# Second layer's attention: later-block sums on VectorE, one triangle product per bank, a bf16 mask, and paired scores

## The chip, the cores and the metric

The kernel runs on one core of one Trainium2 chip. The metric is the device time of one execution in microseconds (us); the median of several runs counts. The core has a matrix engine (TensorE; PE in the profile, PEld for its weight loads), a vector engine (VectorE, DVE), a scalar engine (ScalarE, ACT), GpSimd (POOL) and a queue engine (SyncE, SP) that issues most of the transfers. Matmuls write to PSUM banks of 512 float32 per partition.

## What is computed

Two transformer blocks over 512 tokens of width 1024. The first one (gated linear attention, sliding-window attention and a PEER layer that retrieves single-neuron experts for each token) stays as it is. The change touches the two attentions of the second block, which work on eight stick-breaking heads of width 64 and four differential heads of two scores each:

```python
def one_block(args):                       # stick-breaking, per block of 128 queries
    z = jnp.einsum('bqhd,bkhd->bhqk', qb, k).astype(jnp.float32) * scale
    mask = (k_pos[None, :] < q_pos[:, None])[None, None]
    log_1mb = jnp.where(mask, jax.nn.log_sigmoid(-z), 0.0)
    rem = lax.cumsum(log_1mb, axis=3, reverse=True) - log_1mb
    a = jnp.where(mask, jnp.exp(jax.nn.log_sigmoid(z) + rem), 0.0)
    return jnp.einsum('bhqk,bkhd->bqhd', a.astype(v.dtype), v)

def one_block(args):                       # differential
    logits = jnp.einsum('bqhcd,bkhcd->bhcqk', qb, k).astype(jnp.float32) * scale
    ...
    p = jax.nn.softmax(logits, axis=-1)
    attn = p[:, :, 0] - lam * p[:, :, 1]
    return jnp.einsum('bhqk,bkhd->bqhd', attn.astype(v.dtype), v)
```

Behind the attentions come an output projection, a gated feed-forward of width 2816 and two residual sums.

## The kernel before, in words

Activations lie transposed, features on partitions and tokens along the free axis. The second block is computed in two parts: tokens 0 to 383 as soon as their first block is done (`attend(0, 3, ..., "a", True)`, line 2219), and tokens 384 to 511 later (`attend(3, 4, ub, "b", False)` in `last_block`, line 2197), since the PEER layer gathers the experts of those last 128 tokens row by row (`sparse`, line 1213: indirect transfers issued by POOL, dot products and sums on VectorE, tiles `row` and `vacc`). The weights of part "a" are split into an upper and a lower half (`whi`, `wlo`) and multiplied three times in a reduced format (one record each in the trace); part "b" multiplies in full float32 (two records each).

The order of all instructions is made when the kernel is built. Work is written as generators; a `Weaver` (line 229) always continues the one that its `Model` of the engines (line 70) holds to be ready first, with a handicap given in us where one is set (`(biases(), 8.0)`). A generator gives up its turn at each `yield`; `need(k)` waits for a key that another one sets with `W.set(k)`, `data(t)` for a tile to be loaded. On the chip each engine then works through its instructions in that order, and semaphores make it wait for data and buffers. `stream` (line 1612) feeds the weight tiles: the projections into query, key and value, the output projection and the feed-forward. It takes the pieces of part "b" first when their inputs are there, and else those of "a".

PSUM is laid out in line 1568: two banks `mm` for `stream`, two `w` (scores and transposes of the differential heads, and the sums of squares of all norms, `rstd_bcast`, line 458), two `z` for the stick-breaking scores, one each for the two outputs.

Stick-breaking (`stick`, line 1806): key blocks of 128 are grouped from the last backwards, as many as fit in one bank of 512 columns (`groups`, `offs`, line 1793). In part "a" the blocks 2 and 1 (128 and 256 query columns) make the first group and block 0 (384) the second; in part "b" all four blocks (128 each) make one group. `front` (line 1809) multiplies keys by queries into a bank, and makes the negative log of 1 - beta out of it (ScalarE and VectorE, tile `L`), with a strict mask `sgt` on the diagonal blocks. `back` (line 1830) adds into the same bank, for each key block, a triangle product with its own `L`, a product of all ones with the `L` of every later block, and on diagonal blocks a product of the unit matrix with a mask of -1e30; ScalarE then takes the exponential and the result is multiplied by the values. The core of it:

```python
for jb in jbs:
    o, m = offs[jb]
    PE.matmul(z[:, o:o + m], tri[:, 0], L[h, g][:, o:o + m], stop=False, **kw)
    for j2 in range(jb + 1, b1):
        o2, m2 = offs[j2]
        PE.matmul(z[:, o + m - m2:o + m], tri[:, 1], L[h, where[j2]][:, o2:o2 + m2], stop=False, **kw)
    if 128 * jb >= c0:
        PE.matmul(z[:, o:o + 128], ident, tri[:, 2], stop=True, **kw)
```

Each unit's `front` is emitted ahead of the `back` of the unit before.

Differential (`diff`, line 1874): for a head and a block of 128 queries, `front` (line 1878) multiplies the two 64-feature halves, which lie on partitions 0 to 63 and 64 to 127, each into a `w` bank, with a `yield` between the matmul and VectorE's pass that adds the bias and takes the maximum; `back` (line 1897) normalises, transposes and multiplies by the values. There are 12 units in part "a" (128, 256 and 384 keys for each of four heads) and 4 in part "b" (512 keys).

`biases` (line 1581) loads the position bias of the four heads and masks a corner of each with a memset. `last_feed` (line 2115) is the feed-forward of part "b" and ends the kernel.

## Time and profile before

| | |
|---|---|
| median of 3 runs | 2201.95 us (2199.81 to 2206.16) |
| the profiled execution | 2213.97 us, span from first to last instruction 2212.2 us |
| busy share of the span | PE 91%, PEld 80%, DVE 81%, ACT 44%, POOL 30% |
| instructions | PE 11845, DVE 3705, ACT 1800, POOL 523 |
| mean granted TensorE clock | 0.958 of full speed |
| HBM | 611.54 MB read, 24.38 MB written, 287 GB/s over the span |

All rows come from that one profiled execution. Times are us from the start of the span unless a unit stands beside them. Every instruction carries line 224, that of a helper through which all are recorded, so the rows are told apart by engine, operation and tile: `b_z<-L,tri` is a matmul with `tri` as the stationary and `L` as the moving operand into a bank `b_z`. Matmuls are pipelined: the time that one takes from the engine is the distance of its start to the start of the next, and not its duration.

### The profile page before, as it was taken

The page shows a single profiled execution, that of the slowest core. Times are in us where ns is not written, and L with a number is a line of the kernel's source. Part 1 is how long each engine was busy: PE and PEld are TensorE (multiplying, and loading weights), DVE is VectorE, ACT ScalarE, POOL GpSimd, SP SyncE. Part 2 cuts the span into 40 slices and gives each one's busy share as a digit, 9 for nine tenths or more (in the row PEclk, how much of TensorE's full clock was granted, in tenths as well). Part 3 has the DMA queues.
Part 4 walks back from the last instruction along what each step waited for, and adds up shares of the span by engine and source line. Part 5 has one row for each costly group of instructions (what it writes and reads, how often), then busy time and mean ns, then how long its engine had stood idle before and what let it go on. Part 6 is the DMA issues. An engine that isn't in the chain of part 4 may idle for free.

```text
span 2212.2 us, 33369 instructions
## 1 busy us (share of the span) xinstructions
PE 2014.6 (91%) x11845; PEld 1774.7 (80%) x11845; DVE 1791.9 (81%) x3705; ACT 964.3 (44%) x1800; POOL 656.0 (30%) x523
## 2 busy tenths in 40 slices
PE   2889799798999977899999999799988999999998
PEld 2778676587889866799998998587767999998987
DVE  7846887789999877899898898888889999724577
ACT  1331442212587433444445544444554333344466
POOL 0000222432212234444343344345543555200000
PEclk9899899699999988999999999999999999999999
DMA  9963447898899999999999899688866999742587
GB/s 367 350 210 122 156 137 225 273 334 314 293 312 315 327 326 333 360 391 375 354 370 358 326 394 337 231 299 304 272 218 201 350 375 377 268 156 92 179 285 273
DMA packets 226311, 638.13 MB, mean 288 GB/s; under 512 B 21041, under 2 KB 70465, under 8 KB 226145
## 3 DMA queue, kind: packets, MB, share of 16 engines
q1 hardware_dynamic: 152416, 367.54, 47.0%
q0 software_dynamic: 73728, 268.47, 34.2%
q8 instruction: 93, 1.52, 0.3%
q14 instruction: 74, 0.60, 0.1%
HBM read 611.54 MB, written 24.38 MB: 287 GB/s over the span
## 4 chain that ended last, share of the span: by engine, by line
PE 47%; DVE 22%; DMA 12%; issue 11%; POOL 5%; ACT 2%; SPq 0%; POOLq 0%; DVEq 0%; ACTq 0%
PE b_mm L224 29%; PE b_dacc L224 7%; POOL row L224 5%; DVE row L224 4%; PE b_z L224 4%; PE b_w L224 4%; DMA row<-peer_v,eU 3%; DVE o L224 3%; DMA wraw<-peer_v 3%; DVE vacc L224 2%; DVE wlo L224 2%; PE b_osb L224 1%; DMA row<-w_down 1%; DMA row<-peer_u,eU 1%; PE b_odf L224 1%
## 5 line engine op out<-in xcount | busy, mean ns | idle before, releaser
L224 POOL DMA_INDIRECT row<-peer_u,eU x256 | 328.0, 1281 | 802.0 <-DVE row L224 260.7
L224 POOL DMA_INDIRECT row<-peer_v,eU x256 | 325.2, 1270 | 440.9 <-DVE row L224 198.9
L224 PE MATMUL b_mm<-u,whi 128*128 128x384 f32 x1216 | 326.9, 349 | 11.0 <-ACT u L224 2.4
L224 PE MATMUL b_mm<-h,whi 128*128 128x256 f32 (+2 forms) x1648 | 332.0, 296 | 3.1 <-ACT whi L224 2.4
L224 DVE SCALAR_TENSOR_TENSOR vacc<-row,dots,vacc 128x1024 f32<-128x1024 f32 x254 | 325.2, 1280 | 5.5 <-DMA row<-peer_v,eU 5.0
L224 DVE SCALAR_TENSOR_TENSOR row<-row,h2n 128x1024 f32<-128x1024 f32 x256 | 310.5, 1218 | 10.5 <-DMA row<-peer_u,eU 10.1
L224 PEld LDWEIGHTS b_mm<-h,whi 128*128 128x128 f32 (+1 forms) x1648 | 271.3, 189 | 24.4 <-issue 6.9
L224 PE MATMUL b_mm<-h,wlo 128*128 128x256 f32 (+2 forms) x824 | 242.6, 294 | 13.5 <-DVE wlo L224 13.5
L224 PEld LDWEIGHTS b_mm<-u,whi 128*128 128x128 f32 x1216 | 221.6, 192 | 30.0 <-issue 5.8
L224 PE MATMUL b_mm<-u,wlo 128*128 128x384 f32 x608 | 206.9, 340 | 2.5 <-DVE wlo L224 2.5
L224 ACT ACTIVATE whi<-wraw 128x1024 fp32r<-128x1024 f32 (+3 forms) x129 | 125.5, 973 | 186.9 <-PE b_mm L224 147.1
L224 ACT ACTIVATE vhi<-wraw 128x1024 fp32r<-128x1024 f32 x128 | 135.8, 1062 | 148.6 <-PE b_dacc L224 82.8
L224 PE MATMUL b_dacc<-vhi,ghi 128*128 128x512 f32 x512 | 166.5, 407 | 31.2 <-ACT ghi L224 31.1
L224 PE MATMUL b_mm<-h,uraw 128*128 128x256 f32 x704 | 166.3, 385 | 4.7 <-DMA uraw<-peer_uT 3.3
L224 PEld LDWEIGHTS b_mm<-h,wlo 128*128 128x128 f32 (+1 forms) x824 | 156.1, 189 | 15.9 <-DVE wlo L224 14.8
L224 PE MATMUL b_dacc<-vlo,ghi 128*128 128x512 f32 x512 | 164.4, 403 | 1.4 <-DVE vlo L224 1.4
L224 PE MATMUL b_dacc<-vhi,glo 128*128 128x512 f32 x512 | 162.4, 399 | 0.0
L224 DVE TENSOR_TENSOR vlo<-wraw,vhi 128x1024 fp32r<-128x1024 f32 x128 | 156.2, 1220 | 3.6 <-PE b_dacc L224 2.2
L224 PEld LDWEIGHTS b_mm<-h,uraw 128*128 128x128 f32 x704 | 131.6, 194 | 21.4 <-issue 3.7
L224 DVE TENSOR_TENSOR wlo<-wraw,whi 128x1024 fp32r<-128x1024 f32 (+3 forms) x129 | 143.4, 1113 | 4.2 <-ACT whi L224 2.3
L224 DVE TENSOR_TENSOR wlo<-uraw,whi 128x1024 fp32r<-128x1024 f32 x84 | 103.2, 1229 | 44.3 <-ACT whi L224 42.0
L224 PEld LDWEIGHTS b_dacc<-vhi,ghi 128*128 128x128 f32 x512 | 93.3, 195 | 50.7 <-ACT ghi L224 36.2
(371 smaller groups left out, 3734.4 us busy)
## 6 DMA issues: line engine op xcount, KB each, us to landing
uraw<-peer_uT SPq DMA_DIRECT2D x128, 512.0 KB
wraw<-peer_v SPq DMA_DIRECT2D x128, 512.0 KB
wraw<-w_in SPq DMA_DIRECT2D x60, 512.0 KB
row<-w_ada SPq DMA_DIRECT2D x48, 512.0 KB
wraw<-w_peer_q SPq DMA_DIRECT2D x32, 512.0 KB
gt<-gate_d SPq DMA_DIRECT2D x16, 1024.0 KB
gate_d<-stg SPq DMA_DIRECT2D x16, 896.0 KB
row<-w_in SPq DMA_DIRECT2D x24, 512.0 KB
```

Of the source, the lines that this page charges most:

```text
L224: return f(*args, **kw)
```

## The change

Four edits in the second block's attention, and two that make room.

- Sums of later blocks: in `front`, running sums of `L` over the later key blocks are made on VectorE (tile `Ss`), so that in `back` each key block takes one product of all ones for each piece of the sum in place of one for each later block.
- The triangle product is issued once for the whole bank.
- The mask of -1e30 and the unit matrix it is multiplied by are kept in bf16 (`hide`, `identb`); `biases` converts them, ahead of the bias loads, and `stick` waits for it.
- Both score matmuls of a differential unit are issued one behind the other, into two banks, with one `yield` behind both.
- The tile `fN` of `operands` now lies in the ring `sba`; `tri` has two parts in place of three.

```diff
--- before.py
+++ after.py
@@ -1572,13 +1572,21 @@
     pK = stK.enter_context(tc.tile_pool(name="pK", bufs=1))
     sk, dk = [pK.tile([128, 4, T], F32, name=n) for n in ("sk", "dk")]
     sv, dv = [pK.tile([128, 4, 512], F32, name=n) for n in ("sv", "dv")]
-    tri = pK.tile([128, 3, 128], F32, name="tri")
-    SP.dma_start(tri, A["tri"])
+    tri = pK.tile([128, 2, 128], F32, name="tri")
+    SP.dma_start(tri, A["tri"][:, 0:2])
+
+    hide, identb = [pK.tile([128, 128], BF, name=k) for k in ("hide", "identb")]
+    hide32 = pU.tile([128, 384], F32, name="sqs", bufs=2)[:, :128]
+    SP.dma_start(hide32, A["tri"][:, 2])
     sgt = pK.tile([128, 128], F32, name="sgt")
     SP.dma_start(sgt, A["sgt"])
     bias = pK.tile([128, 4, 512], F32, name="bias")
 
     def biases():
+        yield data(hide32)
+        DVE.tensor_copy(hide, hide32)
+        DVE.tensor_copy(identb, ident)
+        W.set("hide")
         for h in range(4):
             src = bass.AP(tensor=line.tensor, offset=line[h].offset + 127, ap=[[639, 128], [1, 512]])
             SP.dma_start(bias[:, h], src)
@@ -1731,7 +1739,7 @@
                     act(q, x[:, kc], AF.Square)
                     PE.matmul(ps, ones, q, start=(kc == 0), stop=(kc == KC - 1))
                     yield
-                f = pD.tile([128, n], F32, name="fN", bufs=1)
+                f = pD.tile([128, AW], F32, name="sba", bufs=3)[:, :n]
                 act(f, ps, AF.Ln, scale=1.0 / D, bias=eps)
                 act(f, f, AF.Exp, scale=-0.5)
                 yield
@@ -1804,7 +1812,7 @@
         AW = max(w for _, w in groups)
 
         def stick():
-            Z, L, po = {}, {}, {}
+            Z, L, po, later, now = {}, {}, {}, {}, {}
 
             def front(h, g):
                 j, r = h // 2, slice(64 * (h % 2), 64 * (h % 2) + 64)
@@ -1827,20 +1835,31 @@
                         d = l[:, offs[jb][0]:offs[jb][0] + 128]
                         tt(d, d, sgt, OP.mult)
 
+                run = now.setdefault(h, [])
+                for jb in jbs:
+                    o, m = offs[jb]
+                    later[h, jb] = run
+                    new, a0 = [], n - m
+                    for v, a, b in run if jb else ():
+                        t = pD.tile([128, b - a], F32, name="Ss", bufs=2 * max(1, b1 - 2))
+                        tt(t, v, l[:, o + a - a0:o + b - a0], OP.add)
+                        new.append((t, a, b))
+                    e = run[0][1] if run else n
+                    run = ([(l[:, o:o + e - a0], a0, e)] if e > a0 else []) + new
+                now[h] = run
+
             def back(h, g):
                 j, r = h // 2, slice(64 * (h % 2), 64 * (h % 2) + 64)
                 jbs, w = groups[g]
                 z = Z.pop((h, g))
-                where = {jb: gi for gi, (js, _) in enumerate(groups) for jb in js}
                 kw = dict(start=False, skip_group_check=True)
+                PE.matmul(z[:, :w], tri[:, 0], L[h, g], stop=False, **kw)
                 for jb in jbs:
                     o, m = offs[jb]
-                    PE.matmul(z[:, o:o + m], tri[:, 0], L[h, g][:, o:o + m], stop=False, **kw)
-                    for j2 in range(jb + 1, b1):
-                        o2, m2 = offs[j2]
-                        PE.matmul(z[:, o + m - m2:o + m], tri[:, 1], L[h, where[j2]][:, o2:o2 + m2], stop=False, **kw)
+                    for v, a, b in later.pop((h, jb)):
+                        PE.matmul(z[:, o + m - n + a:o + m - n + b], tri[:, 1], v, stop=False, **kw)
                     if 128 * jb >= c0:
-                        PE.matmul(z[:, o:o + 128], ident, tri[:, 2], stop=True, **kw)
+                        PE.matmul(z[:, o:o + 128], identb, hide, stop=True, **kw)
                 yield
                 a = pD.tile([128, AW], F32, name="sba", bufs=3)[:, :w]
                 act(a, z[:, :w], AF.Exp)
@@ -1860,6 +1879,7 @@
             for q in ("sq0", "sk0", "sv0"):
                 yield need(q + tag)
             yield need("xn")
+            yield need("hide")
             yield from front(*units[0])
             for i, (h, g) in enumerate(units):
                 if i + 1 < len(units):
@@ -1880,12 +1900,14 @@
                 p = pD.tile([128, 2, KW], F32, name="dp", bufs=2)
                 m = pD.tile([128, 4], F32, name="dm", bufs=2)
                 P[i, h] = (p, m)
-                for cc in range(2):
+
+                pss = [bank(), bank()]
+                for cc, ps in enumerate(pss):
                     r = slice(64 * cc, 64 * cc + 64)
-                    ps = bank()
                     PE.matmul(ps[:, :nk], dq[r, h, 128 * (i - b0):128 * (i - b0) + 128], dk[r, h, :nk],
                               start=True, stop=True)
-                    yield
+                yield
+                for cc, ps in enumerate(pss):
                     DVE.tensor_tensor_reduce(p[:, cc, :nk], ps[:, :nk], bias[:, h, 512 - nk:], 1.0, -3.0e38,
                                              OP.add, OP.max, m[:, cc:cc + 1])
                 DVE.tensor_scalar(m[:, 0:2], m[:, 0:2], -1.0, None, op0=OP.mult)
```

## Rows read from the trace of the kernel before

**Rows 1.** Busy us by stretch: PE, PEld, DVE, ACT, POOL; clock, DMA share, GB/s

```profile
1469.00:1645.00 176.00, 165.92 (x828) 128.64 (x827) 150.56 (x279) 92.61 (x198) 89.95 (x73) 0.96 0.79 267
...
1700.00:1905.00 205.00, 200.46 (x1150) 198.78 (x1149) 196.56 (x220) 70.01 (x92) 115.70 (x93) 1.00 0.97 357
...
1930.00:2055.00 125.00, 124.40 (x919) 112.70 (x918) 42.31 (x84) 54.60 (x135) 0.00 (x0) 1.00 0.39 123
...
2111.00:2207.00 96.00, 91.91 (x613) 81.71 (x612) 77.66 (x81) 66.74 (x78) 0.00 (x0) 1.00 0.87 303
```

**Rows 2.** TensorE's weight-load queue, what it waited for, 1469 to 1660: us, times, longest

```profile
PEld b_w L224 <- ACT ns L224: 3.3, 3, 2.7
```

**Rows 3.** The same of TensorE's matmuls, 1905 to 2084

```profile
PE b_mm L224 <- DVE wlo L224: 1.5, 3, 0.7
```

**Rows 4.** Matmuls by group, 2055 to 2212: count, busy us, mean ns

```profile
L224 PE MATMUL b_mm<-fh,whi 128*128 128x384 f32 x80 | 20.9, 340 | 0.1
...
L224 PE MATMUL b_mm<-u,whi 128*128 128x384 f32 x35 | 9.1, 339 | 0.0
```

**Rows 5.** Chain of work that ended last: start, us, what

```profile
1470.48 4.39 PE b_mm L224 x24
```

**Rows 6.** TensorE in order of time: start, us to last end

```profile
2084.89 1.05 PE L224 MATMUL b_osb<-ident,xT 128*128 128x128 f32 x8
...
2109.95 0.51 PE L224 MATMUL b_mm<-fh,whi 128*128 128x384 f32 x2
```

**Rows 7.** TensorE in order of time, one head of stretch B

```profile
2000.06 2.17 PE L224 MATMUL b_z<-L,tri 128*128 128x128 f32 x18
2002.07 0.61 PE L224 MATMUL b_mm<-u,row 128*128 128x128 f32 x4
```

**Rows 8.** TensorE in order of time, one score of stretch B

```profile
2019.25 1.12 PE L224 MATMUL b_w<-dk,mix 64*128 64x512 f32 x2
2020.31 0.61 PE L224 MATMUL b_mm<-u,whi 128*128 128x384 f32 x2
```

**Rows 9.** On the tile tri: count, shortest, median, longest ns, first start

```profile
L224 PE MATMUL b_z<-tri,ident x64: 275/275/421, 1476.2 to 2038.8; 128*128 128x128 f32 x64
```

**Rows 10.** TensorE in order of time, stretch A, scores of the differential heads

```profile
1565.70 1.43 PE L224 MATMUL b_w<-dk,mix 64*128 64x384 f32 x4
...
1581.87 0.48 PE L224 MATMUL b_w<-dk,mix 64*128 64x128 f32 x2
1582.29 0.86 PE L224 MATMUL b_osb<-sba,sv 128*64 128x128 f32 x4
...
1627.69 0.49 PE L224 MATMUL b_w<-dk,mix 64*128 64x128 f32 x4
1628.11 0.86 PE L224 MATMUL b_osb<-sba,sv 128*64 128x384 f32 x2
...
1641.44 1.62 PE b_w L224 x2
```

**Rows 11.** Instructions on the tile sgt

```profile
L224 DVE TENSOR_TENSOR L<-L,sgt x32: 285/292/295, 1472.7 to 2032.5; 128x128 f32<-128x128 f32 x32
```

**Rows 12.** SyncE's queue in order of time

```profile
1417.52 1.85 SPq L224 DMA_DIRECT2D bias<-line  x4
1428.18 43.12 SPq L224 DMA_DIRECT2D wraw<-w_in  x8
```

**Rows 13.** Instructions on the tile bias

```profile
L224 DVE CUSTOM_DVE_ANT_0 dp<-b_w,bias x32: 282/488/693, 1479.4 to 2022.9; 128x128 f32<-128x128 f32 x8, 128x256 f32<-128x256 f32 x8, 128x384 f32<-128x384 f32 x8, 128x512 f32<-128x512 f32 x8
...
L224 DVE MEMSET bias<- x4: 112/112/112, 1426.9 to 1448.2; 64x64 f32 x4
```

**Rows 14.** TensorE in order of time, the last expert sum

```profile
1907.22 1.09 PE L224 MATMUL b_w<-ident,vacc 128*128 128x128 f32 x8 [1.02 <-DVE vacc L224]
```

**Rows 15.** VectorE, what it waited for, 1469 to 1660

```profile
DVE L L224 <- ACT sba L224: 9.6, 7, 2.4
DVE dp L224 <- PE b_w L224: 8.3, 8, 2.3
```

## The prediction

> **What bounds the kernel now.** I read the busy time by stretch first [rows 1]. Call 1469 to 1700 us stretch A (attention of the first 384 tokens, beside which the first layer still gathers experts for the last 128) and 1930 to 2055 stretch B (attention of those last 128 tokens). In B TensorE is busy 124.40 of 125.00 us at a granted clock of 1.00, VectorE 42.31: B is TensorE's alone. From 1700 to 1905 TensorE (200.46 of 205), VectorE (196.56) and DMA (share 0.97) are all full. In the attention part of A, 1469 to 1645, TensorE is busy 165.92 of 176.00 us and VectorE 150.56: TensorE leads, but VectorE has only 25.4 us to spare. At the end, 2111 to 2207, DMA moves 303 GB/s at a share of 0.87 and TensorE is busy 91.91 of 96.
>
> Next the waits of TensorE, as its weight-load queue shows them. In A the longest that has a named cause sums to 3.3 us [rows 2], from 1905 to 2084 to 2.4 [rows 3]. So work taken off TensorE in B should come off the end, if something else can fill the engine. What fills it is the feed-forward of the first 384 tokens: after 2055 it still has 80 + 35 matmuls by the upper half of the weights [rows 4] and half as many by the lower, 172 in all; at 4.39 us per 24 [rows 5] that is 31.5 us. The last block's feed begins at 2084.89, and this filler still stands between its matmuls up to 2110 [rows 6]. With 10 to 20 us off there is filler left, and the last feed starts earlier by what was taken.
>
> **Part by part.** A float32 matmul is two records. Eighteen records of 128 columns take 2.01 us to the next group's start [rows 7], so 0.223 us per matmul; 512 columns I put at 4 x 0.213 + 0.01 = 0.86 us (estimate; a 64-row one of 512 columns, alone between other tile shapes, took 1.06 us [rows 8]).
>
> *Triangle products.* In B each of 8 heads has four own-triangle products and six later-block products of 128 columns; after, one own product of 512 columns and three of 128. Saved per head: 10 x 0.223 - 0.86 - 3 x 0.223 = 0.70, in all 5.6 us; with 1.06 for the wide one, 4.0. In A a head goes from 1280 columns in six products to 1152 in five: 0.22 each, 1.8 us.
>
> *Mask.* 64 records [rows 9] are 32 masks, 24 in A and 8 in B, now 0.223 each. No row shows a bf16 matmul. Bounds: 0.06 (a third of a one-record matmul of 384 columns, 4.39 / 24 = 0.183 [rows 5]) and 0.223. I take 0.10, near the one-record row, with a little for the change of type: 0.12 saved each, 2.9 us in A and 1.0 in B; bounds 0 and 5.2 together.
>
> The Trainium skill, in TensorE: Matmul & The Clock Gate, section Wait — 56ns, not 53.3ns?, gives 55.6 ns from start to start for a bf16 matmul of 128 columns at the fast clock; by it the masks would save 32 x 0.167 = 5.3 us (estimate from that page), 1.4 more than I take. No row of this profile shows it.
>
> *Scores side by side.* The trace holds both cases. Two scores of one head that happened to be neighbours took 0.42 us to the next group for four records (1627.69), as long as one alone for two (1581.87) [rows 10]: they use different rows of the array and run at the same time. So the second score of a pair costs nothing where it now costs a visit of its own. B has four such visits of 1.06 us [rows 8]: 4.2 us. Of A's twelve pairs three already ran together, one ran beside another 64-row group, and one overlapped in part (1565.70, some 0.5 us to gain). Seven are apart: two of 128 columns at 0.42, four of 256 at 0.63, one of 384 at 0.84 (on the line between 0.42 and 1.06): 4.2 us, with the half overlap 4.7. Lower bound: 0, if the second waits for its bank.
>
> *Sum on TensorE.* A: 1.8 + 2.9 + 4.7 = 9.4. B: 5.6 + 1.0 + 4.2 = 10.8.
>
> *Added on VectorE.* One add of 128x128 per head in A and two in B. The nearest row, the strict mask's product of the same shape, takes 0.292 us [rows 11]: 2.3 us in A, 4.7 in B, and two small copies. In B VectorE is idle two thirds of the time, and a head's sums are made one unit ahead of its products, so I cost them at nothing; without that cover TensorE would stand 0.6 us per head, 4.7 in all. In A they lie on a nearly full engine.
>
> *The moved step.* The four bias loads and their four memsets now come behind the mask's load and its copy on VectorE; the attention's first products wait for that copy too. The loads were issued at 1417.52, ahead of 43 us in which SyncE's queue issues eight weight loads, each when a buffer comes free [rows 12]; behind these, each can be late by one such step, 5.4 us. The copy holds expert rows behind it if its load is late. The last memset was at 1448 and the first use at 1479 [rows 13], so I cost the step at nothing; uncovered, some 5 us. The normalising factor moves into a ring of three whose third owner after it comes two units later: nothing.
>
> *What comes out.* Of B's 10.8 I count 10.5. In A VectorE must fit 9.4 us less time and 2.3 us more work into its 25 us of spare time, in an order fixed beforehand, beside a granted clock of 0.96. I take two thirds, 6.5; bounds 0 and 9.4. Together 17 us. The profiled execution took 2213.97 us (span 2212.2 and 1.8 around it), so 2197 for it; it lay 12.0 us over the median of 2201.95. For the median: **2185 us**. A measurement of this kernel can tell about 0.3%, 6.6 us, from no change.
>
> **The rivals.**
> (1) All of it comes out, and A's tail gains too, since each pair has one hand-over less: TensorE stood 2.30 us there at 1641.44 [rows 10]. 2202 - 20 - 4 = 2178. Against it: VectorE at 150.56 of 176 us.
> (2) A is VectorE's: the expert rows, for whose last sum TensorE waits at 1907 [rows 14], come no earlier, and 2.3 us of adds go in front. Only B gains: 2202 - 10.8 + 2.3 = 2193. For it: 196.56 of 205 us. Against it: VectorE's idle time in A is mostly waiting for TensorE's scores and what ScalarE makes of them [rows 15].
> (3) The change doesn't do what it says: in the new order the pairs do not overlap, one bank of the two being held. Left are 1.8 + 2.9 in A, two thirds of that 3.1, and 5.6 + 1.0 in B: 9.7, so 2192.
> (4) The planner's new order costs elsewhere nearly what is won: 2200. No row speaks for a place.
> (5) Slower: both "w" banks are asked for at once, in A, where VectorE takes scores out between expert rows of 1.2 us. TensorE issues in order, so a second score without a bank holds everything behind it; a product stood 2.30 us for VectorE's reading of such a bank at 1641.44 [rows 10]. Were each of A's 12 pairs to stand 2.3 us, that is 27.6 us over the forecast: 2213. It turns slower from 17 / 12 = 1.4 us per pair on. Against it: the pair comes behind the value products of the unit before, which wait for the same bank to be read anyway.
>
> The Trainium skill's TensorEngine Tiling (Array Packing), section Gotcha 1: PSUM Pressure, has it that concurrent row tiles need different banks; that is the demand rival (5) rests on, and the 0.42 us pair shows that two banks are free at once at times.
>
> **How the numbers follow.** Chances: forecast 0.46 (2180 to 2190), (1) 0.15, (2) 0.18, (3) 0.08, (4) 0.07, (5) 0.06. Within 0.3% is 2195.3 to 2208.6. Faster: the forecast, (1), and 0.21 of (2) and (3), which lie 2 to 3 us under the border: 0.82. Same: (4) and the other 0.05: 0.12. Slower: 0.06. The range, 2176 to 2198, takes in (1) to (3) with a few us on either side: below, the whole sum with the full mask gain and A's tail (2202 - 26); above, B's lower terms alone (4.0, its pairs and masks nothing). It leaves out (4) and (5).
>
> **What would show it.** Per head of B one own-triangle product of 512 columns and three others, with the mask about 1.6 us where it was eleven times 0.223, 2.45; one record per mask, 0.1 us to the next; the two scores of a pair starting together, and half as many visits. B shorter by 10 us and still full; the last expert row some 6 us earlier than 1907. I am wrong if TensorE's waits for "w" banks in A grow past 10 us, if the last expert row comes no earlier, or if the last feed takes longer than its 122 us from 2085 to 2207 because DMA sets its pace.

## The result, and the profile after

The changed kernel takes **2179.21 us** (median; 2173.12 to 2185.95) where the kernel before took 2204.05 beside it: ratio **0.9887** with a 95% interval of [0.9864, 0.9910], so 25 us less (20 to 30). The forecast was 2185, 17 us less, and the range 2176 to 2198. The profiled execution took 2181.23 us (span 2179.5), so profile against profile it is 32.7 us. The profiled execution of the kernel before was a long one, 10 us over that kernel's median, and 6.9 of the 32.7 us lie ahead of the second layer's first VectorE instruction (1417.6 before, 1410.7 after), in code that the change doesn't touch. Everything below is counted from that instruction on, "the block": 794.6 us before, 768.8 after.

The first view is the busy time by stretch, as in [rows 1]. The stretches are cut at the same events in both kernels: the block's first instruction, the first stick score, the making of the input of the feed-forward of the first 384 tokens (ScalarE's first `u<-sqs`, half a us ahead of the first product with it), the last expert sum, the last feed, the end. The columns are the stretch, its length, the busy time and records of PE, PEld, DVE, ACT and POOL, then the granted clock, the DMA share and GB/s. Before:

```profile
1417.60:2212.20 794.60, 746.55 (x4438) 672.08 (x4438) 607.17 (x911) 367.52 (x650) 239.85 (x192) 0.97 0.75 259
1417.60:1469.60 52.00, 37.52 (x168) 32.98 (x168) 42.97 (x67) 24.08 (x41) 22.48 (x18) 0.84 0.81 275
1469.60:1689.80 220.20, 205.32 (x1036) 163.64 (x1035) 188.14 (x346) 111.50 (x233) 100.52 (x80) 0.96 0.76 254
1689.80:1907.20 217.40, 210.07 (x1182) 205.36 (x1182) 208.53 (x238) 77.02 (x103) 116.85 (x94) 0.99 0.93 343
1907.20:2084.90 177.70, 175.53 (x1267) 162.33 (x1268) 74.65 (x162) 78.77 (x185) 0.00 (x0) 1.00 0.46 150
2084.90:2212.20 127.30, 118.11 (x789) 107.77 (x788) 92.89 (x100) 76.15 (x90) 0.00 (x0) 0.99 0.80 271
```

After, with the stretch of B that answers to 1930 to 2055 of [rows 1] (1918 to 2028):

```profile
1410.70:2179.50 768.80, 722.50 (x4294) 649.92 (x4294) 612.43 (x937) 368.97 (x651) 242.26 (x192) 0.98 0.77 268
1410.70:1458.00 47.30, 35.53 (x168) 31.27 (x168) 40.31 (x66) 22.74 (x37) 19.20 (x16) 0.86 0.78 266
1458.00:1664.40 206.40, 191.54 (x996) 152.80 (x995) 184.98 (x349) 112.05 (x235) 96.54 (x77) 0.99 0.79 264
1664.40:1893.30 228.90, 222.64 (x1242) 217.47 (x1242) 220.31 (x255) 80.50 (x107) 126.52 (x101) 0.98 0.94 347
1893.30:2058.50 165.20, 162.82 (x1153) 148.90 (x1154) 78.71 (x177) 78.03 (x184) 0.00 (x0) 1.00 0.48 155
2058.50:2179.50 121.00, 109.96 (x739) 99.48 (x737) 88.12 (x93) 75.65 (x89) 0.00 (x0) 0.99 0.81 280
...
1918.00:2028.00 110.00, 109.17 (x783) 95.94 (x784) 44.82 (x99) 51.45 (x130) 0.00 (x0) 1.00 0.42 131
```

Read the whole-block row first. TensorE is busy 24.05 us less (746.55 to 722.50) and the block is 25.8 us shorter; what TensorE stands idle is 48.0 us before and 46.3 after. **In this pair of profiles the time went with TensorE's busy time, one for one, and its waits stayed.** Then the stages: the start is 4.7 us shorter, stretch A with its tail 13.8, the expert stage 11.5 *longer*, B 12.5 shorter, the last feed 6.3. A's stage ended 18 us earlier counted from the block's start, yet the last expert sum came only 6.9 us earlier (489.6 to 482.6): the engines are full in the expert stage, and TensorE filled the time it had gained with feed-forward work (1242 records there, 1182 before). That work (the filler of the prediction) was then missing at the end, where it had stood between the last feed's matmuls: in TensorE's order of time it reached to 2110 before, 25 us into the last feed [rows 6], and now ends 12 us into it:

```profile
2058.53 1.05 PE L224 MATMUL b_osb<-ident,xT 128*128 128x128 f32 x8
...
2070.05 0.51 PE L224 MATMUL b_mm<-fh,whi 128*128 128x384 f32 x2
2070.39 0.34 PE L224 MATMUL b_mm<-fh,wlo 128*128 128x384 f32 x1
```

B's new head, in TensorE's order of time (start, us to last end, what), answers to [rows 7, 8]:

```profile
1931.91 1.02 PE L224 MATMUL b_z<-L,tri 128*128 128x512 f32 x2
1932.77 0.22 PE L224 MATMUL b_z<-hide,identb 128*128 128x128 bf16 x1
1932.83 0.44 PE L224 MATMUL b_z<-L,tri 128*128 128x128 f32 x2
1933.10 0.61 PE L224 MATMUL b_z<-Ss,tri 128*128 128x128 f32 x4
1933.64 1.13 PE L224 MATMUL b_w<-dk,mix 64*128 64x512 f32 x4
1934.70 0.71 PE L224 MATMUL b_mm<-u,row 128*128 128x128 f32 x4
```

The wide product takes 0.86 us to the next start, the mask 0.06, the three products behind it 0.81. Of this 0.05 comes with the change of type (the first two records take 0.27 us where two take 0.22 otherwise) and some 0.09 with the change to 64-row tiles behind the last. Then two scores of 512 columns, four records, in 1.06 us: as long as [rows 8] show for one. In A most pairs do the same, as one of 256 columns shows; the pairs at 1591.92 and 1609.23 did not, and their second score ran behind the first:

```profile
1528.95 0.70 PE L224 MATMUL b_w<-dk,mix 64*128 64x256 f32 x4
1529.58 0.86 PE L224 MATMUL b_osb<-sba,sv 128*64 128x384 f32 x2
...
1591.92 1.65 PE L224 MATMUL b_w<-dk,mix 64*128 64x384 f32 x4
...
1609.23 1.44 PE L224 MATMUL b_w<-dk,mix 64*128 64x256 f32 x4
```

Adding up each record of the block from its start to the next one's start (waits taken out) gives TensorE's busy time by kind of work:

```
us of TensorE                     before   after   change   predicted
A: triangle products and mask      24.40   18.57    -5.83    -4.7
A: scores of differential heads    13.28    9.53    -3.75    -4.7
B: triangle products and mask      19.85   13.32    -6.53    -6.6
B: scores of differential heads     8.42    4.24    -4.18    -4.2
A's projections, first feed part  213.90  209.53    -4.37     0
norms in A                         14.98   13.55    -1.43     0
all else                          451.23  453.37    +2.14     0
sum                               746.06  722.11   -23.95   -20.2
```

The row of A's projections counts the split-weight products from the block's start to 1756.3 before and 1728.3 after: A's projections and the first 336 records of its feed-forward. The last three rows have the same instructions in both kernels. Together they shrank by 3.7 us; within A's stage alone such work shrank by 4.2. This goes with the granted clock of A's stage, which rose from 0.96 to 0.99 in the rows above: the lower of the clock's two levels is half the higher (1.2 and 2.4 GHz), so a mean of 0.96 stands for 0.08 of the 220.2 us at the lower one and 0.99 for 0.02 of 206.4. The trace's clock records, which are not rounded, give 16.4 us and 5.4. In the expert stage it went the other way (4.0 us at the lower level before, 8.2 after); over the block it is 40.5 and 29.0 us.

VectorE's new adds took what the strict mask's product takes [rows 11], and the bias loads kept their early place in SyncE's queue, ahead of the weight loads, as in [rows 12]. The adds, on the tile Ss (count, shortest, median, longest ns, first and last start):

```profile
L224 DVE TENSOR_TENSOR Ss<-L x16: 284/290/293, 1462.1 to 2008.9; 128x128 f32<-128x128 f32 x16
L224 DVE TENSOR_TENSOR Ss<-Ss,L x8: 291/292/293, 1928.2 to 2009.3; 128x128 f32<-128x128 f32 x8
```

SyncE's queue in order of time (start, us, what):

```profile
1410.07 0.43 SPq L224 DMA_DIRECT2D sqs<-tri  x1
1410.53 0.43 SPq L224 DMA_DIRECT2D sgt<-sgt  x1
1411.01 1.86 SPq L224 DMA_DIRECT2D bias<-line  x4
1421.45 2.58 SPq L224 DMA_DIRECT2D wraw<-w_in  x2
```

The biases' memsets, on the tile bias:

```profile
L224 DVE MEMSET bias<- x4: 112/112/112, 1423.6 to 1454.5; 64x64 f32 x4
```

Two numbers of the text ahead, the 2.4 us from 1905 to 2084 and the 2.30 us at 1641.44, stand in these lines of the kernel before, the first among the waits of the weight-load queue, the second in TensorE's order of time:

```profile
PEld b_mm L224 <- DVE wlo L224: 2.4, 3, 1.0
```

```profile
1641.44 1.62 PE L224 MATMUL b_w<-ns,ones 128*128 128x384 f32 x2 [2.30 <-DVE dm L224]
```

### The profile page after: what moved, and what is told of

Its sections match the earlier page's. It is cut to its first block, busy times and chain, and to the rows that moved or that the text cites. A ratio compares the mean times of both kernels' runs of the same rounds, so it can differ in the third digit from the quotient of the medians.

```text
span 2179.5 us, 33115 instructions
## 1 busy us (share of the span) xinstructions
PE 1987.3 (91%) x11701; PEld 1748.8 (80%) x11701; DVE 1796.9 (82%) x3731; ACT 964.6 (44%) x1802; POOL 662.3 (30%) x523
## 4 chain that ended last, share of the span: by engine, by line
PE 49%; DVE 21%; DMA 13%; issue 9%; POOL 5%; ACT 2%; SPq 0%; DVEq 0%; POOLq 0%; ACTq 0%
PE b_mm L224 31%; PE b_dacc L224 8%; POOL row L224 5%; PE b_z L224 4%; DMA row<-peer_v,eU 4%; DVE row L224 3%; PE b_w L224 3%; DVE o L224 3%; DVE vacc L224 3%; DMA wraw<-peer_v 3%; DVE wlo L224 2%; DMA row<-w_ada 1%; PE b_osb L224 1%; DMA aR<-act_d 1%; DMA row<-w_up 1%
## 5 line engine op out<-in xcount | busy, mean ns | idle before, releaser
L224 POOL DMA_INDIRECT row<-peer_v,eU x256 | 330.0, 1289 | 436.4 <-DVE row L224 197.8
L224 PE MATMUL b_mm<-u,wlo 128*128 128x384 f32 x608 | 205.3, 338 | 0.4 <-DVE wlo L224 0.4
```

What stands on the lines that cost most here:

```text
L224: return f(*args, **kw)
```

## The experiments

The theory: what TensorE no longer does comes out whole, whichever stretch it is taken from. The rivals here: the gain of A is VectorE's or the early expert rows'; the pair gains by saved hand-overs, not by running at once; the adds cost something. All ratios are against the kernel before, run on the same chip at the same time. First the results together; "A's stage" is the windows row from the first stick score to the making of the feed-forward's input (length, TensorE busy, granted clock), and the last expert sum and the end are counted from the block's start; both come from one profiled execution each. A difference of two of these ratios has an interval of some 7 us to either side (the two half-widths added in squares).

```
                            ratio [95%]              A's stage              last expert  end
before                      1                        220.2  205.3  0.96     489.6        794.6
changed                     0.9887 [0.9864,0.9910]   206.4  191.5  0.99     482.6        768.8
changed, again (11)         0.9890 [0.9868,0.9912]   207.9  192.9  0.98     480.6        764.8
pairs alone (1)             0.9945 [0.9924,0.9966]   209.1  199.2  0.98     490.3        781.5
all, pairs in series (2)    0.9948 [0.9927,0.9968]   214.9  199.8  0.98     485.0        780.3
mask alone (3)              0.9986 [0.9970,1.0002]   222.4  204.4  0.96     478.8        790.7
sums alone (4)              0.9985 [0.9966,1.0005]   213.6  202.3  0.97     486.5        786.6
not in B (5)                0.9931 [0.9909,0.9953]   206.1  191.4  0.99     478.5        773.3
not in A (6)                0.9953 [0.9933,0.9973]   223.3  205.2  0.95     480.6        781.2
adds three times (7)        0.9951 [0.9925,0.9978]   217.2  198.4  0.96     486.5        784.5
all but the mask (8)        0.9894 [0.9860,0.9928]   205.7  197.2  0.98     493.1        771.1
two heads at once (9)       0.9909 [0.9883,0.9935]   214.4  185.0  0.95     470.8        764.9
A's sums on TensorE (10)    0.9927 [0.9901,0.9953]   208.0  192.2  0.99     477.6        774.0
two heads in B alone (12)   0.9867 [0.9840,0.9893]   205.6  189.9  1.00     479.4        760.8
```

**1. Pairs alone.** The kernel before, with the two scores of a head issued next to each other:

```diff
-                for cc in range(2):
+
+                pss = [bank(), bank()]
+                for cc, ps in enumerate(pss):
                     r = slice(64 * cc, 64 * cc + 64)
-                    ps = bank()
...
-                    yield
+                yield
+                for cc, ps in enumerate(pss):
```

> The kernel before with the paired scores alone. Theory 1 (what TensorE no longer does comes off the end, in both stretches): in the profiles of before and after the score visits went from 17.6 to 10.6 us in A and from 8.4 to 4.2 in B, so 11 us less, 2193. Rival 2 (the gain of a pair is its saved hand-over, which shortens A's tail): A's score visits shrink too, but A ends more than 7 us earlier by its own, and the total is 2188 or less. Rival 3 (most of the gain in A came from the planner's new order, not from the parts): within 5 us of 2204, or no relation to the 11 us.

Measured: 2195.56 us, by the ratio 12 us less than before (7.5 to 17); TensorE busy 738.49 us in the block, 8.1 less than before. The pairs' terms of the sum, 4.7 and 4.2, are 8.9. In this profile A's stage ended 11 us earlier from the block's start (260.6 against 272.2) and the last expert sum came no earlier (490.3 against 489.6). So what TensorE saves in A does not bring the expert rows forward, and it comes out all the same. A ended more than 7 us earlier, as rival 2 of this run asks, but the total is not the 2188 or less that it gives; experiment 2 takes the two apart.

**2. Pairs in series.** The changed kernel, with a bf16 product of 128 columns put between the two scores, into the bank that the second score then overwrites:

```diff
                     r = slice(64 * cc, 64 * cc + 64)
+                    if cc:
+                        PE.matmul(ps[:, :128], identb, hide, start=True, stop=True)
                     PE.matmul(ps[:, :nk], dq[r, h, 128 * (i - b0):128 * (i - b0) + 128], dk[r, h, :nk],
```

> The changed kernel with a small 128-row product put between the two scores of a pair (overwritten by the second score), so that the order and the saved hand-over stay and the two can't run at the same time. Theory 1 (the overlap is the gain of the pairs): the visits grow back by 11 us and the 16 small products add about 0.1 us each, 2179 + 13 = 2192. Rival 2 (the hand-over is the gain): within 4 us of 2179.

TensorE in order of time, one pair of B:

```profile
1936.88 1.12 PE L224 MATMUL b_w<-dk,mix 64*128 64x512 f32 x2
1937.93 0.23 PE L224 MATMUL b_w<-hide,identb 128*128 128x128 bf16 x1
1938.09 1.12 PE L224 MATMUL b_w<-dk,mix 64*128 64x512 f32 x2
1939.15 0.60 PE L224 MATMUL b_mm<-u,row 128*128 128x128 f32 x3
```

The pair now takes 2.27 us instead of 1.06, while its two banks are asked for at once, as in the changed kernel. 2194.49 us: 0.9948 against 0.9887, some 13 us given back (7 to 20), of which the 16 small products themselves are some 2.6 (0.16 each). The pair gains by running two scores at once, and rival (3) is refuted from the other side too.

**3. Mask alone.** The kernel before, with the mask in bf16, its load and copy, and the bias loads moved behind them:

```diff
...
-                        PE.matmul(z[:, o:o + 128], ident, tri[:, 2], stop=True, **kw)
+                        PE.matmul(z[:, o:o + 128], identb, hide, stop=True, **kw)
...
+            yield need("hide")
```

> The kernel before with the bf16 mask and the moved loading step alone. Theory 1: the masks cost 6.5 + 1.8 us of TensorE before and 1.1 + 0.5 after, with some 0.05 us of change of type behind each, so 5 us less: 2199. Rival 3 (the order that the moved step brings gives 4.6 us before the first attention product): 2194, and its profile shows the first attention product 47 us behind the first operand product's input, not 52. If the moved step costs something: 2204 or more.

Measured: 2204.90, 3 us less than before; the interval takes in no change and also the 5 us expected. TensorE was busy 4.3 us less in the block (742.23), and the last expert sum came 10.8 us earlier, but TensorE waited 3 us more in A's stage (222.4 less 204.4, against 220.2 less 205.3) and the clock there stayed at 0.96. A gain of the mask alone is not shown.

**4. Sums alone.** The kernel before, with the sums on VectorE and the wide product (the mask and the pairs as before). The part in `front` is that of the change and is left out here; `back` becomes:

```diff
...
+                PE.matmul(z[:, :w], tri[:, 0], L[h, g], stop=False, **kw)
                 for jb in jbs:
                     o, m = offs[jb]
-                    PE.matmul(z[:, o:o + m], tri[:, 0], L[h, g][:, o:o + m], stop=False, **kw)
-                    for j2 in range(jb + 1, b1):
-                        o2, m2 = offs[j2]
-                        PE.matmul(z[:, o + m - m2:o + m], tri[:, 1], L[h, where[j2]][:, o2:o2 + m2], stop=False, **kw)
+                    for v, a, b in later.pop((h, jb)):
+                        PE.matmul(z[:, o + m - n + a:o + m - n + b], tri[:, 1], v, stop=False, **kw)
```

> The kernel before with the wide triangle product and the sums on VectorE alone (float32 mask, scores apart). Theory 1: 1.8 us in A and 5.6 in B off TensorE, the adds hidden: 2197. Rival 4 (the adds are on VectorE's path in A, 2.3 us, and delay the last expert row): 2199 to 2202, with the last expert row not earlier than in the kernel before.

Measured: 2202.76, 3.3 us less than before (0.9966 to 1.0005: from 7.5 less to 1 more). TensorE's busy time fell by 7.8 us, to 738.79, which is the term (1.8 + 5.6 = 7.4). In the profiled execution all of it came out (794.6 to 786.6); in the runs it is less than half, with an interval that takes in all of it and nothing. By itself this can't tell whether the adds cost anything: experiment 7.

**5 and 6. The change in one stretch only.** In experiment 5 B keeps the old products and scores, in experiment 6 A does (the mask is new in both). The edit of experiment 5, with `pair` true for A (in experiment 6 the condition is turned round; the scores of `diff` are switched by the same condition):

```diff
...
-                for jb in jbs:
+                for jb in jbs if pair else ():
...
-                PE.matmul(z[:, :w], tri[:, 0], L[h, g], stop=False, **kw)
+                if pair:
+                    PE.matmul(z[:, :w], tri[:, 0], L[h, g], stop=False, **kw)
```

> The changed kernel with the wide product, the sums and the pairs in part a alone; part b has them as before. The bf16 mask is in both parts. Theory 1 (TensorE's time comes off in both stretches): against after, B's 4.2 of pairs and 5.2 of triangle products come back: 2179 + 9.4 = 2188. The prediction's own count (two thirds of A come out): 2193. Rival (A is VectorE's): no better than the mask alone, 2198 or more.

> The changed kernel with the wide product, the sums and the pairs in part b alone; part a has them as before. The bf16 mask is in both parts. Theory 1: against after, A's 7 us of pairs and 1.2 of triangle products come back: 2187, or a little more if the pairs also shorten the tail of A. Rival (A is VectorE's and its parts gain nothing): within 3 us of 2179.

Experiment 5: 2191.98, 0.9931, which is 9 to 10 us over the changed kernel (0.9887 and 0.9890), with an interval of 3 to 17. B's terms without its mask are 5.6 + 4.2 = 9.8, and in the profile B, from the first product of its input projection to the first of its output projection, takes 125.2 us where the changed kernel takes 115.9: **B's part comes out, as far as the runs can tell, one for one.**

Experiment 6: 2198.27, 0.9953, some 14 us over the changed kernel (8 to 21). A's terms without its mask are 1.8 + 4.7 = 6.5, so **A is worth its terms and more**, some twice as much, where I had taken two thirds. The busy time of A's stage says from where:

```profile
1470.00:1693.30 223.30, 205.22 (x1012) 162.06 (x1011) 192.75 (x351) 112.21 (x234) 104.26 (x85) 0.95 0.76 259
```

Against the changed kernel's row (206.40, 191.54, clock 0.99) the stage is 16.9 us longer: TensorE is busy 13.7 us more, of which 6.5 is the work put back, and idle 3.2 more. The other 7 us go with the clock: by the trace's clock records TensorE had 20.5 us at the lower level there, against 5.4. The runs agree: their mean granted clock over the whole kernel has a median of 0.9615 in experiment 6, 0.963 in the 65 runs of the kernel before beside the experiments, and 0.965 in the ten of the changed kernel.

**7. Adds three times.** The changed kernel with each add written twice more into the same place, 48 adds of 0.292 us, 14.0 us of VectorE, and nothing else:

```diff
                         tt(t, v, l[:, o + a - a0:o + b - a0], OP.add)
+                        tt(t, v, l[:, o + a - a0:o + b - a0], OP.add)
+                        tt(t, v, l[:, o + a - a0:o + b - a0], OP.add)
```

> The changed kernel with each of the 24 sums on VectorE made three times over, so 48 more adds of 0.29 us: 4.7 us more in A and 9.3 in B. Theory 1 (the adds are hidden): 2179, at most 3 more. Rival 4 (VectorE's time in A comes off the end, one for one): 2184; with B's too: 2193.

Busy time by stretch, the whole block, A's stage, and the stretch from the last expert sum to the last feed:

```profile
1414.80:2199.40 784.60, 729.57 (x4294) 654.54 (x4294) 629.29 (x988) 365.68 (x650) 236.99 (x192) 0.97 0.75 263
1461.40:1678.60 217.20, 198.39 (x996) 156.88 (x995) 191.92 (x368) 112.40 (x235) 96.74 (x79) 0.96 0.75 255
...
1901.30:2079.50 178.20, 172.02 (x1184) 156.88 (x1185) 93.15 (x215) 76.18 (x184) 0.00 (x0) 0.98 0.46 151
```

2197.30 us, 0.9951: 14 us over the changed kernel by the ratios (6 to 22). That these 48 adds are hidden is refuted. They cost about as much as they take, but only in part as waits: TensorE does the same matmuls (x4294) in 7.1 us more, at a clock of 0.96 in A's stage and 0.98 in B's, and waits 8.7 us more (55.0 against 46.3). The median clock of these runs is 0.960. In the last of these rows VectorE was busy only 93.15 us of 178.2, and the adds still told: TensorE is idle 6.2 us there, where the changed kernel has 2.4. That the change's own 24 adds cost their 7.0 us is not shown by this; it would go with what experiment 4 lacks.

**8. All but the mask.** The changed kernel with the old float32 mask and the old loading order:

```diff
-                        PE.matmul(z[:, o:o + 128], identb, hide, stop=True, **kw)
+                        PE.matmul(z[:, o:o + 128], ident, tri[:, 2], stop=True, **kw)
...
-            yield need("hide")
```

> The changed kernel with the float32 mask and without the moved loading step. Theory 1: TensorE's 5 us of masks come back: 2184. Rival 3 (the order that the moved step brings is worth 4.6 us before the first attention product): 2189, and the first attention product stands 52 us behind the first operand's input again, not 47.

2187.08, 0.9894 [0.9860, 0.9928], beside 0.9887 and 0.9890: the mask's 3.9 us is within the interval, and so is nothing. Its profile shows both sides: TensorE is busy 729.50 us, 7.0 more than in the changed kernel, and idle 4.8 less (41.5). The last expert sum comes 10.5 us later (493.1 against 482.6), the mirror of experiment 3, and this costs the end next to nothing (771.1 against 768.8).

**9 and 12. Further along the same line.** Two neighbouring heads' stick scores use different rows of the array, and their value products different columns. Experiment 9 issues both side by side, in A and B; experiment 12 in B alone (it is the changed kernel in A). The core of the edit:

```diff
-            def front(h, g):
+            def front_mm(j, g):
...
+                for h in hs:
+                    Z[h, g] = bank("z")
                 for jb in jbs:
                     o, m = offs[jb]
...
+                    for h in hs:
+                        r = slice(64 * (h % 2), 64 * (h % 2) + 64)
+                        PE.matmul(Z[h, g][:, o:o + m], sk[r, j, 128 * jb:128 * jb + 128], sq[r, j, q0(jb) - c0:],
+                                  start=(jb == jbs[0]), stop=True, skip_group_check=True)
...
+            def values(j, g):
...
+                    for h in (2 * j, 2 * j + 1):
+                        r = slice(64 * (h % 2), 64 * (h % 2) + 64)
+                        PE.matmul(po[j][r, n - m:n], sv[:, jb, 64 * h:64 * h + 64], E[h][:, o:o + m],
+                                  start=(jb == b1 - 1), stop=(jb == 0), skip_group_check=True)
```

> The changed kernel with the stick-breaking scores of two heads (rows 0 to 63 and 64 to 127) and their value products (columns 0 to 63 and 64 to 127) issued side by side as well, two heads per unit. The two z banks then belong to one unit, so the next unit's scores wait for both exponentials. Theory 1 (the time is TensorE's busy time behind the first block plus some 47 us of waits that stay): the 64-row scores cost 13.2 + 8.7 us and the value products 12.7 + 8.1; side by side each would cost half, so up to 21 us less, 2158, if the waits stay. If only row tiles run together and column tiles don't: 2168. Rival (the units' chain through ScalarE and VectorE becomes the pace, with both banks taken): the waits grow by more than 10 us and A ends later; 2170 to 2190.

A's stage in experiment 9:

```profile
1457.40:1671.80 214.40, 185.01 (x996) 150.63 (x995) 193.04 (x359) 111.12 (x235) 105.49 (x84) 0.95 0.79 271
```

2188.24, 0.9909: no gain over the changed kernel, though TensorE was busy 16.3 us less in the block (706.21). In A's stage it is busy 6.5 us less and idle 29.4 instead of 14.9, at a clock of 0.95. The profiled execution was the shortest of its runs, 11 us under their median; the runs' clock has a median of 0.9595. TensorE's two longest named waits in A's attention (1457.4 to 1651.8), and the longest for ScalarE's part of the stick-breaking scores:

```profile
PE b_w L224 <- DVE dp L224: 6.1, 3, 5.2
PE b_w L224 <- DVE dm L224: 4.6, 3, 2.6
...
PE b_z L224 <- ACT sba L224: 1.4, 2, 1.0
```

The rival's number is right: the waits grew by more than 10 us and A's stage got longer. Its mechanism, the chain of the stick-breaking units through ScalarE, is not what the named waits show: the longest are for VectorE's work on the differential heads (4.1 and 0.7 us in the changed kernel). Why this order brings them was not tested.

> The changed kernel with two heads side by side (scores and value products) in part b alone; part a as in the change. In the run with both parts that way the 64-row scores of B went from 8.7 to 4.4 us and the value products from 8.1 to 4.2, with waits of TensorE in B under 2 us more, while A lost 14 us to waits. Theory 1: 8 us less than the change, ratio about 0.985 to 0.986 against the kernel before, and TensorE's waits from the second block's start at 44 to 48 us. Rival (the unit's chain sets B's pace and the gain goes into B's length): ratio 0.989, as the change.

2177.61, 0.9867 [0.9840, 0.9893]. It is the lowest ratio here, 5 us under the changed kernel, with overlapping intervals: not shown to be faster. B's heads in TensorE's order of time, two heads' scores and later two heads' values:

```profile
1964.76 1.16 PE L224 MATMUL b_z<-mix,sk 64*128 64x128 f32 x16
1965.85 0.71 PE L224 MATMUL b_mm<-u,row 128*128 128x128 f32 x4
...
1967.38 1.09 PE L224 MATMUL b_osb<-sba,sv 128*64 128x128 f32 x16
1968.41 0.49 PE L224 MATMUL b_w<-ns,ones 128*128 128x128 f32 x2
```

Sixteen records of scores go in 1.09 us and sixteen of values in 1.03, as long as one head's eight took. TensorE's busy time in the block fell to 710.75, by 10 to 12 us, of which its waits took back 4 to 6 (50.0 us idle; forecast were 44 to 48).

**10. A's sums back on TensorE.** The changed kernel, with A's later-block products as they were and its 8 adds left out:

```diff
-                for jb in jbs:
+                for jb in () if pair else jbs:
...
+                    for j2 in range(jb + 1, b1) if pair else ():
+                        o2, m2 = offs[j2]
+                        PE.matmul(z[:, o + m - m2:o + m], tri[:, 1], L[h, where[j2]][:, o2:o2 + m2], stop=False, **kw)
```

> The changed kernel with the later blocks' products of part a on TensorE as before (8 adds fewer on VectorE, 1.8 us more on TensorE); the wide product stays, and part b keeps its sums. The tripled adds cost 18 us for 48 adds. Theory 1 (adds hidden): 2181. Rival 4 (adds in A cost more than their own time, since TensorE waits and its clock falls): 2174 to 2177.

2192.69, 0.9927, slower than the changed kernel by 8 to 9 us where the same or a gain was expected; the intervals overlap by a little. The idea that A's adds cost more than they save is not supported. Why it is slower is open: the profiled execution was at 2184.38, 8 us under its own median, so its profile (723.52 us busy, 50.5 idle) does not show the runs' loss. The clock does not show it either: its median over these runs, 0.965, is that of the changed kernel.

**11. The changed kernel again**, unchanged, on the chip of experiments 9 and 10:

> The changed kernel once more beside the other two. Theory 1: 2179, with 46 us of waits of TensorE from the second block's start and 25 to 32 us at the lower clock, as in its first profile. If the 10 us less of lower clock in A was chance of that execution, 35 to 41 us at the lower clock in the new profile.

2184.39, 0.9890 [0.9868, 0.9912], beside 0.9887: the result repeats. Its profile shows what can differ between two executions of one kernel: the block took 764.8 us against 768.8, with 720.65 busy and 44.2 idle. TensorE had 29.7 us at the lower level in the block, as forecast (29.0 in the first profile), so the lower figure was not chance of that one execution. In the profiles of the kernels that have at most one of the three edits (products, mask, pairs) in A (before, 1, 3, 4, 6) it is 36.4 to 42.3 us; in those that have more of them 22.6 to 31.3, but for the tripled adds (41.0) and the two heads in A (42.0).

## Why the prediction was right

The forecast of 2185 stood 6 us over the median; the sign, TensorE's sum and the mechanism (its busy time comes off the end) held. But 17 us less were forecast and 25 (20 to 30) measured: the part of the sum that I let come out was too small. In the two profiles the 25.8 us of the block are 20.3 of TensorE's terms, 3.8 by which the work that the change doesn't touch got shorter (680.6 to 676.8; 675.4 in the repeat), and 1.7 of waits. Point by point:

- **TensorE's sum.** 9.4 + 10.8 = 20.2 predicted; the four rows of the table above come to 9.6 and 10.7, 20.3. In B each term is as worked out: the wide product at the low end of its two bounds (0.86), the pair at nothing extra, the mask between its bounds. The mask takes 0.06 and 0.05 more behind it, 0.11 where I took 0.10. The Trainium skill, TensorE: Matmul & The Clock Gate, section Wait — 56ns, not 53.3ns?, agrees on the mask itself (55.6 ns; here 1932.77 to 1932.83); the estimate by it of 5.3 us saved is too large for this kernel by the change of type behind the masks, which it leaves out. In A the pairs gave 3.75 instead of 4.7, since two of the twelve still ran one score behind the other; the products and mask gave 5.8 instead of 4.7, some of that by the clock. That the sum came out so close is in part luck of these two.
- **B comes out.** Predicted 10.5; from the first product of its input projection to the first of its output projection B went from 126.6 to 115.9 us and stayed full (109.17 busy of 110.00). Experiment 5 gives 9 to 10 for 9.8, within wide bounds.
- **"What comes out", A at two thirds: the step that failed.** I let 6.5 of A's 9.4 us come out, held back by VectorE's 25 us of spare time. Experiment 6 puts A, its mask not counted, at some 14 us (8 to 21) for 6.5 of terms. Two things were missing. What TensorE saves in A need not bring the expert rows forward: A's stage ends earlier, the time goes to feed-forward work, which is then gone from the end, so it comes out whole. And A's stage ran at a higher granted clock, 0.99 and 0.98 against 0.96, in which the work there that the change doesn't touch took 4.2 us less. I had read 0.96 off [rows 1] and used it only as a brake. Why the clock rose is not shown.
- **The last expert row.** Predicted some 6 us earlier, measured 6.9 from the block's start: the right number by luck, for a wrong reason. The kernels with the moved loading step have their last expert sum at 470.8 to 486.5 us, those without at 486.5 to 493.1; the pairs alone moved it not at all, the mask with its loading step alone by 10.8. And it is not worth its time at the end (experiments 3 and 8). What of the step does it was not separated: with it the first stick score came 46.5 to 49.4 us after the block's start, without it 50.0 to 52.7.
- **The moved step** at nothing: the loads stayed ahead of the weight loads (1411.01), and the last memset ended 11 us before the biases' first use at 1465.9. Its price held, its side effect I had not seen.
- **The adds** at nothing: not refuted for the 24 of the change, and doubtful. Twice that number more cost about their own time (experiment 7), in B also, where I had named the cover. My sum has them at 0 and A's clock at 0; if both are errors, they are of opposite sign.

The rivals: (1), 2178, is nearest the median, but its reason, fewer hand-overs in A's tail, is not what is seen: TensorE's waits in the block went only from 48.0 to 46.3 us. (2) is right in that TensorE's gain brings no expert rows forward and wrong in what follows from it. (3) is refuted by the 1.06 us for four records. (4) does not show in the changed kernel; experiment 10 may be a case of it. For (5), these are the waits in question in A after the change (1458 to 1650):

```profile
DVE mix L224 <- ACT nr L224: 6.8, 6, 1.9
PEld b_w L224 <- DVE dp L224: 5.4, 3, 2.0
...
DVE L L224 <- ACT sba L224: 2.5, 2, 1.6
...
PEld b_w L224 <- ACT ns L224: 2.2, 1, 2.2
...
DVE dp L224 <- PE b_w L224: 1.6, 4, 0.7
```

The wait for a "w" bank that VectorE still reads is there, 5.4 us in three waits. It was there before too, though [rows 2] do not show it:

```profile
PEld b_w L224 <- DVE dp L224: 3.0, 2, 1.9
```

It grew, and stays under the 10 us that would have made me wrong. VectorE's own waits for ScalarE's `sba` and for the scores fell from 9.6 and 8.3 us [rows 15] to 2.5 and 1.6; that for the norm factor `nr` grew from 3.3 to 6.8.

The last feed, the third thing that could have proved me wrong, fell from 127.3 to 121.0 us as its filler ran out 13 us earlier. DMA, at a share of 0.81 now, did not set its pace: TensorE stood idle 11.0 us in it, 9.2 before, while ScalarE's waits for the weights' loads went from 18.6 to 21.7 us.

## What to carry to other kernels

Where an engine is full over several stages and has work that can be moved between them, price a saving on it at its whole busy time and look for it where the filler ends, not in the stage where it was saved; check it on the whole-block row, busy time and idle time apart. It holds as long as the waits stay: in experiment 9 TensorE was busy 16 us less and nothing came of it. In a stage whose mean granted clock is under 1.00, a few us saved came here with as much again by the clock (experiment 6), and work added on another engine lost as much (experiment 7). Take an edit off alone as well as on alone, and know the interval: the mask and the sums, each alone, gave 3 us, where the runs could tell neither from nothing nor from their terms of 3.9 and 7.4, while the whole gave 25 (20 to 30) for 20.2.

## What was not expected of the hardware

- Two float32 products that fill different columns of the array (128x64 tiles, two heads' values into one bank) run at once too: with pairs of heads issued together, the value products of the block fell from 20.9 us to 10.6 (12.74 + 8.14 to 6.46 + 4.17), the stick scores (64-row tiles) from 21.9 to 12.1.
- The mean granted clock of A's stage lay between 0.95 and 1.00 over these kernels, which do nearly the same matmuls there. It was lowest, 0.95, where TensorE stood idle for 29.4 and 18.1 us (experiments 9 and 6), but idle time alone does not order it: 8.5 and 15.7 us went with 0.98 and 1.00 (experiments 8 and 12). What sets it stays open.
- 14.0 us of adds on an engine that was 80% busy in the block cost the whole kernel 14 us (6 to 22); in the profiled execution, 15.8 us longer in the block, TensorE's same matmuls took 7.1 us more and its waits 8.7.
